# Second products' weights in column pieces, pair 13 combined on the chip, rows read back in pair 14, second norm around two rows

## The chip, the cores and the metric

The kernel runs on one core of one Trainium2 chip. The metric is the device time of one execution in microseconds (us). The kernel before took 1079.23, 1079.86 and 1081.11 us in three runs, median 1079.86 us. The engines are TensorE (PE, its weight loads PEld), VectorE (DVE), ScalarE (ACT), GpSimd (POOL) and SyncE (SP), which here only issues DMAs.

## The reference, cut to what matters

One encoder layer over 512 tokens of 1024 columns in float32: three token mixers, a projection, a first LayerNorm, a mixture of 32 experts, a second LayerNorm. The change lies in the experts and the second norm:

```python
lg = (xt @ wg) + bg; gsel = argmax(lg); p_top = softmax(lg)[gsel]     # one of 4 groups
top_l, top_i = top_k(le_of_that_group, 2)                             # two of its 8 experts
wts = softmax(top_l) * p_top
hdn = silu(xb @ w1[e]) * (xb @ w3[e]); yb = hdn @ w2[e]               # 1024 -> 512 -> 1024
y[token] += yb * wts                                                  # two experts a token
x = LN(alpha * x + y) * ln2_g + ln2_b
```

Each expert has w1 and w3 (1024x512) and w2 (512x1024), 2 MB each. All 32 experts are loaded: 96 blocks, 201 MB.

## The kernel before, in words

Experts go in 16 pairs. A pair's 2x64 token slots stand side by side on TensorE's columns, `q` being the expert of the pair. The blocks come in the order of `seq`: w1 of pair p, w2 of pair p-1, w3 of pair p; at the end w1 and w3 of pair 15, then w2 of 14, then w2 of 15. SP issues their DMAs in that order into a ring of seven slots, each block into the slot that the block seven before it leaves (`load_expert`, L1026; `loads`, L1020). The last eight blocks are loaded in pieces (L1055 to L1060): halves, and four column pieces of w2 of pair 15. In DRAM a w2 block is one row of 4 x 1024 numbers a partition, so a piece of 256 columns is four runs of 1 KB, a piece of 512 columns four runs of 2 KB.

For each pair `pr` (loop L1530) the code emits: `first_product` with w1 (`gate`; between its matmuls 3 and 4 of eight the four transposes of the pair before, `second_product`, L1328), `product` of the pair before with its w2 in two halves of 512 columns (L1413), `put_rows` (POOL scatters that pair's rows to `yd` in DRAM, L1405), `first_product` with w3 (`up`), `gated` (ACT L1321, DVE L1322). Every second pair gathers the next four experts' tokens (`onehots`, `gather`). `XG`, `xnh`, `xnl` are the tokens' rows and their gathered form; `yacc` is the sum for each token.

Pairs 0 to 13 go through `yd`. After pair 14's `gated` stand `overflow()` (a branch over all engines at L1343, not taken here, for experts with more than 64 tokens) and `collect()`: POOL reads `yd` back in eight DMAs of 512 KB (L1279) into the place of `xnh` and `xnl`, and DVE adds each, weighted, to `yacc` (L1282). Pairs 14 and 15 don't go through DRAM: `back` turns the weighted one-hot matrix `Pw` (PE L1314, DVE L1316, L1317), `product` evacuates as a high and a low part (ACT L1422, DVE L1423), and `combine` multiplies them by the one-hots into token order (L1434), which DVE adds to `yacc` (L1438, or L1443 with a sum for the norm). Pair 14's second half is combined within the same accumulation as pair 15's pieces 2 and 3.

The second norm: ACT squares each piece of each token tile t (L1449; the very last tile on DVE, L1446, L1447), `second_scale` makes mean and 1/sd (L1472 to L1475), and `second_norm` scales (ACT L1484), multiplies by the gain `g2` (DVE L1485), adds the offset `b2` (L1487: half of them on POOL, half on DVE) and sends the half row out (SP L1488). `second_rows` (L1457) spreads gain and offset over 128 partitions with 16 fp32 products of 128 columns on PE before pair 15's `up`.

A scheduler of the framework sets each engine's order: by the place in the code, but an instruction that its own timing says could run in a gap is drawn ahead. Each engine then runs its list in order.

Of the kernel before, what the change touches and what calls it, by code (L numbers as in the profile page):

```python
# [72 lines left out]
def _host(inp):  # L73
# [83 lines left out]
def body(tc, T):  # L157
# [847 lines left out]

    def block(i):

        if i == 7:
            return lambda n: lambda c, cs=slice(None): quarter(i, c)[:, cs]
        if i == 8:  # L1010
            return lambda n: lambda c, *cs: quarter(i, c // 2)[:, c % 2 * 512:c % 2 * 512 + 512]
        return lambda n: lambda c, cs=slice(None): reg(slot(i), n, 4096 // n)[:, c, cs]
# [13 lines left out]
    def load_expert(i=None):  # L1026
        if i is None:
            i = nl_[0]
            nl_[0] += 1
        if i < len(seq):  # L1030
            o = slot(i)
            if i == 6:
                pass
            elif i in (7, 8):

                if i == 8:
                    for p in range(4):
                        for k in (7, 8):
                            sp.dma_start(quarter(k, p), T[seq[k][0]][seq[k][1]][:, 1024 * p:1024 * p + 1024])
            elif 9 <= i <= 20:  # L1040

                lone = i in (9, 14)
                old = i - 7 - (i < 14)
                wide = 1024 if seq[old][0] == "moe_w2" else 4096
                if lone or i % 2 == (i < 14):
                    m = wide // (4 if i < 12 else 2)
                    for o in range(0, wide, m):
                        for k in (i,) if lone else (i - 1, i):
                            view = lambda v: v.rearrange("p (f n) -> p f n", n=wide)[:, :, o:o + m]
                            sp.dma_start(view(reg(slot(k), 4096)), view(T[seq[k][0]][seq[k][1]]))  # L1050
            elif i < len(seq) - 8:
                return sp.dma_start(reg(o, 4096), T[seq[i][0]][seq[i][1]])
            elif i % 2:

                n = 1024 if seq[i][0] == "moe_w2" else 4096  # L1055
                for cs in PIECES if i == len(seq) - 1 else [slice(0, n // 2), slice(n // 2, n)]:
                    for k in (i - 1, i):
                        sp.dma_start(reg(slot(k), 4096 // n, n)[..., cs] if n < 4096 else reg(slot(k), n)[:, cs],
                                     T[seq[k][0]][seq[k][1]].rearrange("p (f n) -> p f n", n=n)[..., cs]
                                     if n < 4096 else T[seq[k][0]][seq[k][1]][:, cs])  # L1060
# [235 lines left out]
    def first_product(pr, w, between=None):  # L1296

        so = 128 * (pr % 2)
        ph = pt("as", 2)
        for c in range(8):  # L1300
            if c == 4 and between:
                between()
            for q in range(2):
                pe.matmul(ph[64 * q:64 * q + 64], XG[:, c, so + 64 * q:so + 64 * q + 64], w[q](8)(c),  # L1304
                          start=(c == 0), stop=(c == 7), tile_position=(0, 64 * q))
        return ph
# [24 lines left out]
    def overflow():  # L1331
# [6 lines left out]
        wv = reg(slot(place[14, "moe_w3", 1]), 4096)  # L1338
# [4 lines left out]
        with tc.If(nv > 0), tc.For_i(0, nv, 1):  # L1343
# [34 lines left out]
            w2 = wv.rearrange("p (f n) -> p f n", f=4)  # L1378
            for hf in range(2):
                cs = slice(hf * 512, hf * 512 + 512)  # L1380
                py = pt("pj", 3)[:64]
                for f in range(4):
                    pe.matmul(py, ht[:, f], w2[:, f, cs], start=(f == 0), stop=(f == 3))
# [11 lines left out]
    n2 = [reg(slot(place[15, "moe_w1", 1]) + 1024 * i, 1024) for i in range(2)]  # L1395
    g2, b2 = n2
# [11 lines left out]
    def product(pr, cs, w, PT_=None, ws=None):  # L1408

        py = pt("pj", 3)[:, :cs.stop - cs.start]  # L1410
        for f in range(4):
            for q in range(2):
                pe.matmul(py[64 * q:64 * q + 64], hT[pr % 2][:, f, 64 * q:64 * q + 64], w[q](4)(f, cs),  # L1413
                          start=(f == 0), stop=(f == 3), tile_position=(0, 64 * q))
        if pr < 14:
            if cs.start:
# [8 lines left out]
    def combine(pr, cs, PT_, ws):  # L1425

        terms = [(PT_, v) for v in (yb14 if pr == 14 else yb)]
        if pr == 15 and cs.start >= 512:
            terms = [(turned_[14][0], v) for v in yb14] + terms
        for t in range(4):  # L1430
            pc = (pt("as", 2), pt("ao", 1), pt("as", 2), pt("g", 2))[t]
            pc = pc[:, :cs.stop - cs.start]
# [6 lines left out]
            else:  # L1439

                k = PIECES.index(cs)
                n = cs.stop - cs.start
                dve.scalar_tensor_tensor(ya, pc, 1.0, ya, op0=OP.mult, op1=OP.add, accum_out=bnp[:, t, k, 1:2])  # L1443
                if k == len(PIECES) - 1 and t == 3:
                    d = sil[1][:, (t % 2) * n:(t % 2) * n + n]
                    dve.tensor_scalar(d, ya, -float(n), bnp[:, t, k, 1:2], op0=OP.mult, op1=OP.add)  # L1446
                    dve.scalar_tensor_tensor(d, d, 1.0, d, op0=OP.mult, op1=OP.mult, accum_out=bnp[:, t, k, 2:3])  # L1447
                else:
                    act.activation(junk[:, :n], ya, AF.Square, scale=-float(n), bias=bnp[:, t, k, 1:2],  # L1449
                                   accum_out=bnp[:, t, k, 2:3])  # L1450
                if k == len(PIECES) - 1:
                    second_scale(t)
        if pr == 15 and k == len(PIECES) - 1:
            for t in range(4):
                second_norm(t)

    def second_rows():  # L1457

        for i in range(4):
# [4 lines left out]
            act.activation(n2[i // 2][:, 512 * (i % 2):512 * (i % 2) + 512], p.rearrange("p a b -> p (a b)"), AF.Copy)  # L1464
# [4 lines left out]

    def second_scale(t):  # L1470
# [4 lines left out]
        dve.scalar_tensor_tensor(sm[:, t, 0:1], mv[:, t, 0:1], -1.0 / n, mv[:, t, 1:2], op0=OP.mult, op1=OP.mult)  # L1475

    def second_norm(t):
        for hf in range(2):
            cs = slice(hf * 512, hf * 512 + 512)
            v = yacc[:, t, cs]  # L1480
            if t == 0 and hf == 0:
                dve.tensor_scalar(v, v, mv[:, t, 1:2], sm[:, t, 0:1], op0=OP.mult, op1=OP.add)  # L1482
            else:
                act.activation(v, v, AF.Identity, scale=mv[:, t, 1:2], bias=sm[:, t, 0:1])  # L1484
# [45 lines left out]
    for pr in range(16):  # L1530
# [9 lines left out]
        after = second_rows() if pr == 15 else None  # L1540
        with tc.issue_after(after.ins) if after else nullcontext():
            up = first_product(pr, w[2:4])
        gated(sil[pr % 2], gate, up)
        if pr >= 14:
            turned_[pr] = back(pr)
        if pr == 14:
            overflow()
            collect()
        loads(pr, "moe_w3")
        if pr % 2 and pr < 15:  # L1550
            for t in range(4):
                onehots(pr // 2 + 1, t)
                if pr == 13:
                    weighted(7, t)
# [3 lines left out]
        if pr == 0:  # L1558
            overflow_places()
    evacuated = turned_slots(15)()  # L1560
# [3 lines left out]
    product(14, halves[0], blocks(14)[4:], *turned_[14])  # L1564
    combine(14, halves[0], *turned_[14])
    product(14, halves[1], blocks(14)[4:], *turned_[14])
    for i in range(len(PIECES) + 1):
        if i < len(PIECES):
            product(15, PIECES[i], blocks(15)[4:], *turned_[15])
        if i:  # L1570
            combine(15, PIECES[i - 1], *turned_[15])
    ctx.close()
# [16 lines left out]
```

## Time and profile before

| | us |
|---|---|
| three runs, lowest / median / highest | 1079.23 / 1079.86 / 1081.11 |
| the profiled execution | 1079.46 |
| its span | 1077.5 |
| PE / DVE / ACT / POOL busy | 994.0 / 442.5 / 315.7 / 198.6 |

The profiled execution's time is 1.96 us above its span, and 0.40 us under the median. Times in rows are microseconds from the start of the span. "Busy" of PE counts overlapping matmuls once; the distance of two starts is the better measure of its pace. A row of DMA queues tells packets, MB and the share of 16 DMA engines' time that the packets took. `q1` is SP's queue (weights), `q0` POOL's (rows of `yd`).

### The profile page before, as it was taken

Reading aid. Unit: us, or ns where it says so; the run is one execution under the profiler, and the core shown is the slowest. Engines: PE = TensorE matmul, PEld = TensorE weight load, DVE = VectorE, ACT = ScalarE, POOL = GpSimd, SP = SyncE. Lnnn points to the kernel's source line nnn. Section 1 sums busy time; section 2 is a strip of 40 time slices with the busy share of each in tenths; the row PEclk is TensorE's granted clock in tenths of the full one; section 3 lists DMA queues with packets and bytes.
Section 4 is the critical chain, followed back from the end, with each engine's and each line's share of the span. In section 5 each row is a group of like instructions: output and inputs, shape, how many; then the busy total and the mean of one; then the engine's idle time right before and its main releaser. Section 6 shows DMA issues by size and latency. Waiting matters only on the chain. (4 is left out here: it accounts for less than half of the span.)

```text
span 1077.5 us, 13175 instructions
## 1 busy us (share of the span) xinstructions
PE 994.0 (92%) x5118; PEld 646.1 (60%) x5118; DVE 442.5 (41%) x950; ACT 315.7 (29%) x655; POOL 198.6 (18%) x184
## 2 busy tenths in 40 slices
PE   7989996999999999999998999899989898989973
PEld 5778775977677788888775344434443443334432
DVE  5767893256763533334484221222020210201157
ACT  6873231255653332244133010101010100101115
POOL 1531651222232100233042400000000000000102
PEclk9999998999999999999998999999999999999987
DMA  9422213311114223435465999999999999999982
GB/s 340 165 91 69 84 74 83 113 56 44 59 40 155 81 78 117 196 118 206 175 234 212 382 396 422 428 405 418 429 428 429 428 427 427 428 427 425 404 309 78
DMA packets 52048, 266.04 MB, mean 247 GB/s; under 512 B 15228, under 2 KB 19964, under 8 KB 34832
## 3 DMA queue, kind: packets, MB, share of 16 engines
q1 hardware_dynamic: 47696, 254.67, 59.9%
q0 software_dynamic: 3424, 8.02, 1.9%
q10 hardware_dynamic: 864, 2.49, 0.7%
q8 instruction: 41, 0.67, 0.2%
q14 instruction: 23, 0.19, 0.0%
HBM read 254.13 MB, written 14.61 MB: 249 GB/s over the span
## 5 line engine op out<-in xcount | busy, mean ns | idle before, releaser
L1304 PE MATMUL as<-m,m 128*64 128x512 f32 x1024 | 245.8, 608 | 12.9 <-DMA m<-moe_w 12.9
L1304 PEld LDWEIGHTS as<-m,m 128*64 128x64 f32 x1024 | 77.1, 140 | 154.8 <-issue 133.1
L373 PE MATMUL pj<-m_4096r,m_2048r 128*128 128x512 f32 x400 | 158.2, 396 | 4.4 <-POOL m_2048r L268 2.4
L371 PE MATMUL pj<-m_4096r,m_1024r 128*128 128x512 f32 x400 | 161.0, 402 | 0.0
L372 PE MATMUL pj<-m_4096r,m_1024r 128*128 128x512 f32 x400 | 157.3, 393 | 0.0
L1413 PE MATMUL pj<-m,m 128*64 128x512 f32 (+1 forms) x544 | 128.6, 581 | 5.3 <-DMA m<-moe_w 5.3
L268 DVE TENSOR_TENSOR m_2048r<-m,m_1024r 128x1024 fp32r<-128x1024 f32 x67 | 76.4, 1140 | 98.6 <-ACT m_1024r L267 98.4
L267 ACT ACTIVATE m_1024r<-m 128x512 fp32r<-128x512 f32 (+1 forms) x74 | 68.3, 923 | 138.1 <-PE pj L372 119.8
L1413 PEld LDWEIGHTS pj<-m,m 128*64 128x64 f32 x544 | 45.6, 140 | 79.4 <-issue 67.6
L373 PEld LDWEIGHTS pj<-m_4096r,m_2048r 128*128 128x128 f32 x400 | 75.6, 189 | 21.5 <-POOL m_2048r L268 3.3
L371 PEld LDWEIGHTS pj<-m_4096r,m_1024r 128*128 128x128 f32 x400 | 75.7, 189 | 19.6 <-issue 4.3
L1417 DVE COPY m<-pj 128x512 f32<-128x512 f32 x14 | 9.7, 692 | 186.8 <-PE pj L1413 153.6
L372 PEld LDWEIGHTS pj<-m_4096r,m_1024r 128*128 128x128 f32 x400 | 75.7, 189 | 14.4 <-issue 0.2
L1405 POOL DMA_INDIRECT yd<-m,m x14 | 13.5, 966 | 370.9 <-DVE m L1417 304.2
L1190 PE MATMUL g<-m_1024r,m_4096r 128*128 128x256 f32 x232 | 58.6, 293 | 0.0
L1191 PE MATMUL g<-m_1024r 128*128 128x256 f32 x232 | 56.9, 284 | 0.0
L754 POOL TENSOR_SCALAR m<-m,m 128x128 f32<-128x128 f32 (+3 forms) x32 | 35.8, 1127 | 91.6 <-DVE m L753 85.7
L1290 ACT ACTIVATE m<-g,m 128x256 f32<-128x256 f32 x29 | 16.4, 564 | 121.1 <-PE g L1191 73.5
L1322 DVE TENSOR_TENSOR m<-m,as 128x512 f32<-128x512 f32 x16 | 11.0, 687 | 99.0 <-PE as L1304 99.0
L1190 PEld LDWEIGHTS g<-m_1024r,m_4096r 128*128 128x128 f32 x232 | 44.3, 191 | 6.7 <-issue 6.5
L1329 ACT ACTIVATE m<-g 128x512 f32<-128x512 f32 x16 | 9.6, 597 | 126.4 <-PE g L1328 126.4
L1191 PEld LDWEIGHTS g<-m_1024r 128*128 128x128 f32 x232 | 44.5, 192 | 0.0
(372 smaller groups left out, 1501.3 us busy)
## 6 DMA issues: line engine op xcount, KB each, us to landing
m<-moe_w SPq DMA_DIRECT2D x73, 2048.0 KB, 22.0
m<-wm SPq DMA_DIRECT2D x33, 1024.0 KB, 4.8
m<-moe_w SPq DMA_DIRECT2D x30, 1024.0 KB, 13.7
m<-moe_w SPq DMA_DIRECT2D x32, 512.0 KB, 7.7
yd<-m SPq DMA_DIRECT2D x4, 1024.0 KB, 8.2
m<-wo SPq DMA_DIRECT2D x2, 2048.0 KB, 10.3
m<-yd POOLq DMA_DIRECT2D x8, 512.0 KB, 12.5
m<-xT SPq DMA_DIRECT2D x8, 256.0 KB, 5.5
```

What stands on the lines that cost most here:

```text
L267: act.activation(r32(hi), src, AF.Copy)
L268: lo_engine[0].tensor_tensor(r32(lo), src, hi, op=OP.subtract)
L371: pe.matmul(out, r32(wh(c)), r32(mh(c)), start=(c == 0), stop=False)
L372: pe.matmul(out, r32(wh(c)), r32(ml(c)), start=False, stop=False)
L373: pe.matmul(out, r32(wl(c)), r32(mh(c)), start=False, stop=(c == n - 1))
L754: pool.tensor_scalar(s_[:, :n], s_[:, :n], st[:, 1:2], None, op0=OP.mult)
L1190: pe.matmul(o, r32(xnh[:, t, c * 128:c * 128 + 128]), r32(Pm[:, t]), start=(t == 0), stop=False)
L1191: pe.matmul(o, r32(xnl[t][:, c * 128:c * 128 + 128]), r32(Pm[:, t]), start=False, stop=(t == 3))
L1290: act.activation(XG[:, c], o, AF.Identity, scale=ln1g[:, c:c + 1], bias=ln1b[:, c:c + 1])
L1304: pe.matmul(ph[64 * q:64 * q + 64], XG[:, c, so + 64 * q:so + 64 * q + 64], w[q](8)(c), start=(c == 0), stop=(c == 7), tile_position=(0, 6 ...
L1405: pool.indirect_dma_start(out=yd, out_offset=bass.IndirectOffsetOnAxis(ap=tabs.bitcast(I32)[:, pr, 0:1], axis=0), in_=ybf[pr % 2], in_offs ...
L1413: pe.matmul(py[64 * q:64 * q + 64], hT[pr % 2][:, f, 64 * q:64 * q + 64], w[q](4)(f, cs), start=(f == 0), stop=(f == 3), tile_position=(0, ...
```

## The change

w2 stands in DRAM as four pieces of 256 columns, each one contiguous run of 4 KB a partition; every load of a part of a block is now contiguous. Pair 0's second product runs in four pieces. Pair 13 no longer goes through `yd`: it is turned (`back(13)`) and combined on the chip, in pair 14's place of the loop, with two halves of eight matmuls and eight DVE adds. `overflow` moves from pair 14 to pair 12. `collect` is cut in two: the reads are issued at the end of pair 13 (behind its `gather`), the additions stand at the end of pair 14. A DMA of 8 KB brings gain and offset as two rows (`gb2`). `second_rows` spreads the gain alone; `back(15)` goes ahead of `up`. At the end pair 14's product runs in four pieces, and each half of pair 14 is combined by itself.

In the second norm the gain is multiplied into `yacc` piece by piece before the scale is known (`gained`), and the scale -mean/sd and a row of ones are turned on PE, and multiplied by the two rows: `offset - mean/sd * gain` comes from PE in PSUM, and one DVE instruction finishes a half row. ACT squares all 16 pieces; the last four squares, the scales and the norms are emitted in turn.

```diff
-        a["moe_w2"][0].reshape(32, 4, 128, 1024).transpose(0, 2, 1, 3).reshape(32, 128, 4096))
+        a["moe_w2"][0].reshape(32, 4, 128, 4, 256).transpose(0, 2, 3, 1, 4).reshape(32, 128, 4096))
+    d["ln2gb"] = np.ascontiguousarray(np.concatenate([a["ln2_g"], a["ln2_b"]], axis=0))
...
-                n = 1024 if seq[i][0] == "moe_w2" else 4096
-                for cs in PIECES if i == len(seq) - 1 else [slice(0, n // 2), slice(n // 2, n)]:
+                n = 1024 if i > len(seq) - 5 else 2048
+                for o in range(0, 4096, n):
                     for k in (i - 1, i):
...
+                        sp.dma_start(reg(slot(k), 4096)[:, o:o + n], T[seq[k][0]][seq[k][1]][:, o:o + n])
...
         for t in range(4):
             for j in range(2):
                 pool.dma_start(rows[j][t], yd[512 * j + 128 * t:512 * j + 128 * t + 128])
+        yield
...
-        if pr == 15 and cs.start >= 512:
-            terms = [(turned_[14][0], v) for v in yb14] + terms
...
+    def gained(k, ts=range(4)):
+        for t in ts:
+            ya = yacc[:, t, PIECES[k]]
+            dve.tensor_tensor(ya, ya, g2[:, PIECES[k]], op=OP.mult)
...
     def second_scale(t):
...
+        yield
         dve.reciprocal(mv[:, t, 1:2], mv[:, t, 1:2])
+        dve.scalar_tensor_tensor(ms[:, t, 0:1], mv[:, t, 0:1], -1.0 / n, mv[:, t, 1:2], op0=OP.mult, op1=OP.mult)
+        p = pt("g", 2)[0:2, 0:128]
+        pe.transpose(p, ms[:, t], ident)
+        act.activation(rows2[:, t], p, AF.Copy)
+        yield
     def second_norm(t):
         for hf in range(2):
             cs = slice(hf * 512, hf * 512 + 512)
+            p = pt("pj", 3)
+            pe.matmul(p, rows2[:, t], gb2[:, cs], start=True, stop=True)
             v = yacc[:, t, cs]
-            dve.tensor_tensor(v, v, g2[:, cs], op=OP.mult)
-            e = pool if hf == 0 else dve
-            e.tensor_tensor(v, v, b2[:, cs], op=OP.add)
+            dve.scalar_tensor_tensor(v, v, mv[:, t, 1:2], p, op0=OP.mult, op1=OP.add)
             sp.dma_start(ov[:, t, cs], v)
...
         if 0 < pr < 15:
-            for cs in halves:
-                product(pr - 1, cs, blocks(pr - 1)[4:])
-            put_rows(pr - 1)
+            for cs in PIECES if pr == 1 else halves:
+                product(pr - 1, cs, blocks(pr - 1)[4:], *turned_.get(pr - 1, ()))
             loads(pr - 1, "moe_w2")
+            if pr < 14:
+                put_rows(pr - 1)
+            else:
+                for cs in halves:
+                    combine(pr - 1, cs, *turned_[pr - 1])
+        if pr == 15:
+            second_rows()
+            turned_[pr] = back(pr)
...
-        if pr == 14:
+        if pr == 12:
             overflow()
-            collect()
...
+        if pr == 13:
+            rows_ = collect()
+            next(rows_)
+            pool.dma_start(gb2, T["ln2gb"])
+        if pr == 14:
+            drain(rows_)
+    last = [lambda cs=cs: product(14, cs, blocks(14)[4:], *turned_[14]) for cs in PIECES]
+    last[0]()
     evacuated = turned_slots(15)()
...
+    last[1]()
+    last[2]()
     combine(14, halves[0], *turned_[14])
+    last[3]()
     for i in range(len(PIECES) + 1):
         if i < len(PIECES):
             product(15, PIECES[i], blocks(15)[4:], *turned_[15])
+        if i == 0:
+            combine(14, halves[1], *turned_[14])
+        else:
             combine(15, PIECES[i - 1], *turned_[15])
+            if 1 < i < len(PIECES):
+                gained(i - 2)
...
+    for t in range(4):
+        next(scales[t])
+        if t < 2:
+            gained(2, (t + 2,))
+        gained(3, (t,))
+        next(scales[t])
+        if t:
+            second_norm(t - 1)
+    second_norm(3)
```

## Rows read from the trace of the kernel before

**Rows 1.** Windows: us, busy and count of each engine, granted clock, DMA share, GB/s.
```profile
900.00:950.00 50.00, 44.96 (x232) 20.56 (x231) 9.15 (x20) 4.73 (x9) 1.92 (x2) 1.00 1.01 427
...
1027.50:1033.10 5.60, 0.00 (x0) 0.00 (x0) 4.07 (x5) 0.00 (x0) 0.00 (x0) 0.77 1.03 396
1034.20:1049.20 15.00, 14.22 (x71) 6.60 (x70) 7.09 (x11) 3.93 (x6) 0.00 (x0) 0.90 0.84 274
1048.00:1050.00 2.00, 2.00 (x16) 1.36 (x12) 0.69 (x2) 0.63 (x2) 0.00 (x0) 1.00 0.03 12
1049.20:1059.40 10.20, 10.20 (x81) 8.05 (x80) 6.89 (x33) 8.39 (x28) 0.00 (x0) 1.00 0.00 0
1059.40:1074.00 14.60, 0.00 (x0) 0.00 (x0) 14.12 (x30) 7.44 (x17) 6.59 (x4) 0.68 0.29 108
1074.00:1077.50 3.50, 0.00 (x0) 0.00 (x0) 0.00 (x0) 0.00 (x0) 0.00 (x0) 0.50 0.41 152
```

**Rows 2.** Timeline of PE, pairs 14 and 15: start, us, what, count, idle before.
```profile
989.66 0.66 PE L1314 MATMUL g<-m,m 128*128 128x128 f32 x4
...
1013.03 0.74 PE L1328 MATMUL g<-m,m 128*128 128x128 f32 x4 [1.97 <-PEq L1343]
...
1015.27 1.81 PE L1463 MATMUL g<-m 128*128 128x128 f32 x8
1016.91 1.06 PE L1463 MATMUL pj<-m 128*128 128x128 f32 x8
...
1018.79 7.09 PE L1304 MATMUL as<-m,m 128*64 128x512 f32 x32
...
1033.19 1.09 PE L1328 MATMUL g<-m,m 128*128 128x128 f32 x4 [5.72 <-DVE m L1322]
1034.20 5.17 PE L1413 MATMUL pj<-m,m 128*64 128x512 f32 x16
1040.15 0.50 PE L1434 MATMUL as<-m_1024r,m_512r 128*128 128x512 f32 x1 [0.78 <-ACT m_1024r L1422]
...
1041.89 0.40 PE L1434 MATMUL g<-m_1024r,m_512r 128*128 128x512 f32 x1
...
1050.39 1.95 PE L1413 MATMUL pj<-m,m 128*64 128x256 f32 x16
...
1058.76 0.64 PE L1434 MATMUL g<-m_1024r,m_512r 128*128 128x256 f32 x4
```

**Rows 3.** Timeline of POOL and DVE around the rows read back from `yd`.
```profile
1013.41 4.40 POOL L1279 DMA_DIRECT2D m<-yd  x8 [13.64 <-PEq L1343]
1021.04 1.28 DVE L1282 SCALAR_TENSOR_TENSOR m<-m,m,m 128x1024 f32<-128x1024 f32 x1 [16.05 <-DMA m<-yd]
...
1032.36 0.68 DVE L1322 TENSOR_TENSOR m<-m,as 128x512 f32<-128x512 f32 x1
```

**Rows 4.** DMA queues in 960 to 980 and in 985 to 1005.
```profile
q1 hardware_dynamic: 576, 8.41, 98.6%
...
q0 software_dynamic: 85, 0.20, 2.5%
```

**Rows 5.** DMA queues in 1020 to 1030, then in 1036 to 1048.
```profile
q0 software_dynamic: 727, 2.65, 67.4%
q1 hardware_dynamic: 690, 1.38, 36.3%
...
q1 hardware_dynamic: 3472, 3.47, 88.2%
```

**Rows 6.** Timeline of DVE and ACT in the last stage.
```profile
1042.24 0.68 DVE L1438 TENSOR_TENSOR m<-m,ao 128x512 f32<-128x512 f32 x1
...
1050.54 0.41 DVE L1443 SCALAR_TENSOR_TENSOR m<-ao,m 128x256 f32<-128x256 f32 x1
...
1052.44 0.51 ACT L1449 ACTIVATE m<-m,m 128x256 f32<-128x256 f32 x1
...
1068.76 4.01 DVE L1485 TENSOR_TENSOR m<-m,m 128x512 f32<-128x512 f32 x3
```

More of the change, by code (lines that the diff above doesn't have):

```diff
@@ L1004, in quarter, with w2_columns @@
         return reg(RING[2] + 1024 * k if i == 7 else woh[1][k], 1024)
+    def w2_columns(v, f, cs):
+        k0, k1 = cs.start // 256, cs.stop // 256
+        return v[:, k0, f] if k1 == k0 + 1 else v[:, k0:k1, f]
     def block(i):
-        if i == 7:
-            return lambda n: lambda c, cs=slice(None): quarter(i, c)[:, cs]
+        if seq[i][0] == "moe_w2":
+            if i == 7:
+                return lambda f, cs: shaped(quarter(i, cs.start // 256), 4, 256)[:, f]
+            return lambda f, cs: w2_columns(reg(slot(i), 4, 4, 256), f, cs)
         if i == 8:
-            return lambda n: lambda c, *cs: quarter(i, c // 2)[:, c % 2 * 512:c % 2 * 512 + 512]
-        return lambda n: lambda c, cs=slice(None): reg(slot(i), n, 4096 // n)[:, c, cs]
+            return lambda c: quarter(i, c // 2)[:, c % 2 * 512:c % 2 * 512 + 512]
+        return lambda c: reg(slot(i), 8, 512)[:, c]
     def blocks(pr):
@@ L1042, in load_expert @@
                 lone = i in (9, 14)
-                old = i - 7 - (i < 14)
-                wide = 1024 if seq[old][0] == "moe_w2" else 4096
                 if lone or i % 2 == (i < 14):
-                    m = wide // (4 if i < 12 else 2)
-                    for o in range(0, wide, m):
+                    m = 4096 // (4 if i < 12 else 2)
+                    for o in range(0, 4096, m):
                         for k in (i,) if lone else (i - 1, i):
-                            view = lambda v: v.rearrange("p (f n) -> p f n", n=wide)[:, :, o:o + m]
-                            sp.dma_start(view(reg(slot(k), 4096)), view(T[seq[k][0]][seq[k][1]]))
+                            sp.dma_start(reg(slot(k), 4096)[:, o:o + m], T[seq[k][0]][seq[k][1]][:, o:o + m])
             elif i < len(seq) - 8:
@@ L1382, in overflow @@
                 for f in range(4):
-                    pe.matmul(py, ht[:, f], w2[:, f, cs], start=(f == 0), stop=(f == 3))
+                    pe.matmul(py, ht[:, f], w2_columns(w2, f, cs), start=(f == 0), stop=(f == 3))
                 act.activation(r32(yb[0][:64, cs]), py, AF.Copy, scale=ws)
@@ L1393, in overflow @@
             dve.tensor_scalar(cnt[:, 1:2], cnt[:, 1:2], 64.0, None, op0=OP.add)
-    n2 = [reg(slot(place[15, "moe_w1", 1]) + 1024 * i, 1024) for i in range(2)]
-    g2, b2 = n2
+    g2 = reg(slot(place[15, "moe_w1", 1]), 1024)
+    gb2 = reg(MSB, 1024)[0:2]
     ov = T["out"].rearrange("(t p) d -> p t d", p=128)
@@ L1412, in product @@
             for q in range(2):
-                pe.matmul(py[64 * q:64 * q + 64], hT[pr % 2][:, f, 64 * q:64 * q + 64], w[q](4)(f, cs),
+                pe.matmul(py[64 * q:64 * q + 64], hT[pr % 2][:, f, 64 * q:64 * q + 64], w[q](f, cs),
                           start=(f == 0), stop=(f == 3), tile_position=(0, 64 * q))
-        if pr < 14:
-            if cs.start:
+        if pr < 13:
+            if cs.start % 512 or cs.start and cs.stop - cs.start == 512:
                 dve.tensor_copy(ybf[pr % 2][:, cs], py)
@@ L1427, in combine @@
         terms = [(PT_, v) for v in (yb14 if pr == 14 else yb)]
-        if pr == 15 and cs.start >= 512:
-            terms = [(turned_[14][0], v) for v in yb14] + terms
+        n = cs.stop - cs.start
         for t in range(4):
-            pc = (pt("as", 2), pt("ao", 1), pt("as", 2), pt("g", 2))[t]
-            pc = pc[:, :cs.stop - cs.start]
+            pc = pt(*((("pj", 3), ("ao", 1), ("pj", 3), ("g", 2)) if pr == 13 else
+                      (("as", 2), ("ao", 1), ("as", 2), ("g", 2)))[t])[:, :n]
             for i, (m, v) in enumerate(terms):
@@ L1439, in combine @@
             else:
-                k = PIECES.index(cs)
-                n = cs.stop - cs.start
+                k = cs.start // n
                 dve.scalar_tensor_tensor(ya, pc, 1.0, ya, op0=OP.mult, op1=OP.add, accum_out=bnp[:, t, k, 1:2])
[L1444 to L1455, printed above, removed]
+                act.activation(junk[:, :n], ya, AF.Square, scale=-float(n), bias=bnp[:, t, k, 1:2],
+                               accum_out=bnp[:, t, k, 2:3])
+    def gained(k, ts=range(4)):
+        for t in ts:
+            ya = yacc[:, t, PIECES[k]]
+            dve.tensor_tensor(ya, ya, g2[:, PIECES[k]], op=OP.mult)
     def second_rows():
-        for i in range(4):
+        for i in range(2):
             p = pt("g", 2, 4, 128) if i % 2 else pt("pj", 3, 4, 128)
@@ L1468, in body @@
     junk = sil[0]
+    ms = small(4, 2)
+    rows2 = reg(slot(place[15, "moe_w1", 1]) + 1024, 4, 128)[0:2]
     def second_scale(t):
@@ L1535, in body @@
         if 0 < pr < 15:
-            for cs in halves:
-                product(pr - 1, cs, blocks(pr - 1)[4:])
-            put_rows(pr - 1)
+            for cs in PIECES if pr == 1 else halves:
+                product(pr - 1, cs, blocks(pr - 1)[4:], *turned_.get(pr - 1, ()))
             loads(pr - 1, "moe_w2")
-        after = second_rows() if pr == 15 else None
-        with tc.issue_after(after.ins) if after else nullcontext():
-            up = first_product(pr, w[2:4])
+            if pr < 14:
[6 more added lines that the diff above has]
+            turned_[pr] = back(pr)
+        up = first_product(pr, w[2:4])
         gated(sil[pr % 2], gate, up)
-        if pr >= 14:
+        if pr in (13, 14):
             turned_[pr] = back(pr)
-        if pr == 14:
+        if pr == 12:
             overflow()
-            collect()
         loads(pr, "moe_w3")
@@ L1552, in body @@
                 onehots(pr // 2 + 1, t)
-                if pr == 13:
-                    weighted(7, t)
+                if pr > 10:
+                    weighted(pr // 2 + 1, t)
             gather()
@@ L1563, in body @@
     dve.memset(bnp[:, :, :, 0:1], float(PIECES[0].stop))
-    product(14, halves[0], blocks(14)[4:], *turned_[14])
+    dve.memset(ms[:, :, 1:2], 1.0)
+    last[1]()
+    last[2]()
     combine(14, halves[0], *turned_[14])
-    product(14, halves[1], blocks(14)[4:], *turned_[14])
+    last[3]()
     for i in range(len(PIECES) + 1):
@@ L1569, in body @@
             product(15, PIECES[i], blocks(15)[4:], *turned_[15])
-        if i:
+        if i == 0:
+            combine(14, halves[1], *turned_[14])
+        else:
             combine(15, PIECES[i - 1], *turned_[15])
+            if 1 < i < len(PIECES):
+                gained(i - 2)
+    scales = [second_scale(t) for t in range(4)]
+    gained(2, (0, 1))
+    for t in range(4):
[7 more added lines that the diff above has]
+    second_norm(3)
     ctx.close()
```

16 lines of the change are left out of this document (4 added, 12 removed).

## The prediction

> **What bounds the kernel now.** I read the windows first, by stage, then PE's timeline at the end, then the DMA queues. In the expert stage the weights bound: from 900 to 950 the 16 DMA engines are full (share 1.01, 427 GB/s) while PE is busy for 44.96 of 50 us [rows 1]. So work added to PE, DVE, ACT or POOL before the last pairs is free up to about 5 us in 50, and so is the branch's stop of PE (1.97 us). The DMA bytes are not free anywhere.
>
> At the end the bound changes three times [rows 1]. From 1027.5 to 1033.1 PE does nothing and the DMA engines are full. From 1034.2 PE is the bound: 14.22 of 15.0 us, then 10.20 of 10.20, while the DMA share falls to 0.84 and 0. From PE's last product (1059.4, its last row in [rows 2]) to 1074.0 DVE is busy for 14.12 of 14.60, and 3.5 us follow for the last row's way out. The chain of waits shows only this last part. So three things count: when PE can start the last products (call it S, 1034.20 in [rows 2]), how long it needs from S to its end E (25.2 us to 1059.40), and what follows E (18.1 us). These give the span of 1077.5; the profiled execution took 1.96 us more, and it lies 0.40 us under the median.
>
> **Step 1, the stream and S.** PE's 5.72 us are a wait for `gated(15)` [rows 2], which stood on DVE behind six additions of rows from `yd`: the first waited for 16.05 us, and L1322 ran at 1032.36 though `up` had ended at 1025.9 [rows 2, 3]. The reads had been issued at 1013.41, behind the branch [rows 3]. In the new order they go out near 981, behind pair 13's gather, so this wait goes, and with it the branch's 1.97 us and half of `second_rows`. What is late next is the weights themselves: the 4.19 MB of reads pass ahead of w3 of pair 15 instead of behind it.
>
> When do the weights end? Their last data moved at 1048 (from there the DMA share is 0.03 [rows 1]). Packets of 16 KB move at 8.41 MB / (0.986 x 20 us) = 426 GB/s [rows 4], of 4 KB at 2.65 / 6.74 = 393, of 2 KB at 1.38 / 3.63 = 380, of 1 KB at 3.47 / 10.6 = 328 [rows 5]. Pair 15's w2 (4.19 MB) goes from 1 KB to 4 KB packets: 12.8 to 10.7 us, -2.1. Pair 14's, from 2 KB to 4 KB: -0.4. Pair 13's scatter is no more: -0.5 (2.5% of 20 us [rows 4]). Up to three early blocks get larger packets: at most 6.3 MB x (1/380 - 1/426) = -1.8 us, nothing if slots were late there; I take -0.5. The data then end at 1044.5. Behind w3 of pair 15 lie 8.39 MB at 393 GB/s, 21.3 us, so its data end at 1023.2; with 1 us until this is known and half of `up` (7.09 us [rows 2]) behind it, S is 1027.8 at best. PE waits for weights in this stretch. After the idle stretch at 1027.5 its granted clock was 0.77 over that window, so part of it at the lower level of 1.2 GHz, where four fp32 products of 128 columns take 1.64 us (1015.27 to the next group's start at 1016.91) instead of 0.89 (1.06 less the same overlap of 0.17) [rows 2]. One such stretch in `gate` or `up` costs about 2 us. I take S = 1030, bounds 1027.8 and 1033.
>
> Hidden in this stage: pair 13's two halves of combining (2 x 2.1 us of PE, and eight adds of 0.6 on DVE [rows 2, 6]), its turn (0.66), the extra one-hots, pair 0's quarter pieces (4 x 1.9 instead of about 7.1, +0.5), the branch at pair 12. The cover is the 5 us in 50 and the longer DMA time of pairs 14 and 15. SP passes the branch with four or five blocks of 2 MB still in flight (4.9 us each at 427), so the stream should not run dry there; a dry stream would cost its whole idle time, 0 to 5 us, and I take 0.
>
> **Step 2, S to E.** Eight pieces at 1.9 (1.95 with the last one's end) are 15.2; pair 14's halves 2 x 2.14 (eight products from 1040.15 to 1042.29) 4.3; pair 15's four combinings of half the columns 4 x 1.07, 4.3; the turn 0.7; the last evacuation's wait, mostly covered by the piece before, 0.2 (0.78 uncovered) [rows 2]. Sum 24.7, 0.5 less than before. DVE and ACT keep up, just: a piece of pair 15 costs DVE some 3.0 us with the gain (four adds with sum at 0.34 apart, four products as long, an evacuation), PE 2.95, ACT 3.05. E = 1054.7.
>
> **Step 3, E to the end.** POOL leaves. In [rows 6] three products by the gain take 4.01 us on DVE beside POOL, against 0.60 a piece when DVE is alone (four adds of 0.68 start 0.60 apart). From E on DVE's own sum is now 1.4 (four sums) + 2.6 (eight gains of 256 columns) + 1.8 (small ones) + 8 x 0.62 = 10.8 us. But two other chains are longer. ACT squares all 16 pieces at some 0.65 (0.51 and a read of the sum, [rows 6]) and starts when the first sums of pair 15 exist, 7.4 us before E; with two evacuations that is 11.3 us, so its last square ends at E + 3.9. Root, reciprocal, product, transposition and copy, each a hop of 0.2 to 0.4, follow; I take 1.7. At E + 5.6 PE begins eight fp32 products of 512 columns. Their moving operand has two rows, but 512 columns are four times 128: 0.89 each at 2.4 GHz and 1.64 at 1.2 [rows 2]. PE has stood still for 5 us by then, as before 1033. I take two at the lower level, two half and half, four at the upper: 3.3 + 2.5 + 3.6 = 9.4; transpositions between them 0.5; the last DVE instruction 0.7; the way out 3.5. The sum is E + 19.7. Bounds: all at the upper level E + 17.4, all at the lower E + 23.4, and DVE alone, if PE kept ahead, E + 14.3.
>
> The rule of the Trainium skill that speaks against this step is in "TensorE: Matmul & The Clock Gate", section "Why this matters for your kernels": idle gaps between bursts of matmuls bring the clock back to its lower level. The trace agrees (granted 0.68 over 1059.4 to 1074.0, 0.50 after [rows 1]). It changes the mix of the eight products, no bound.
>
> **Sum.** 1054.7 + 19.7 = 1074.4, against 1077.5: S -4.2, S to E -0.5, behind E +1.6. With 1.96 the profiled execution would take 1076.4; on the scale of the median 0.4 more: 1076.8.
>
> **Rivals.**
>
> *The reads hold `gated(14)` (slower).* DVE's additions stand in the code behind `gated(14)`, but they need only pair 13's combining, some 7 us earlier, so the scheduler may draw them ahead; it did so with pair 14's turn, which runs at 989.66 inside pair 13's product [rows 2]. On the chip the reads are slow there: when both queues had work they moved one packet for one (727 and 690 [rows 5]). 1024 packets of 4 KB are 64 for each DMA engine; beside 16 KB packets one takes 0.62 + 0.17 us, beside 8 KB ones 0.31 + 0.17. From 981, 22 pass with w3 of pair 14 until 998, the other 42 with the halves of w1 and w3 of pair 15 until about 1018. If six additions stand ahead, as they did before L1322, the sixth ends near 1012 and w1's second half comes no earlier than that: nothing lost. If all eight do, `gated(14)` ends at 1020.5, then come the turn, half of `gate` (3.5), `second_rows` and `back` (3.4), `up` (7.1) and one stretch at the lower level: S = 1037, E = 1061.7, and with the same tail and the same 2.4 a time of 1083.8. It decides from the point at which L1322 of pair 14 starts later than 1014. For it: the same instructions stopped DVE before. Against: it takes the last two of eight. Chance 0.2.
>
> The skill's "DMA: Bandwidth & Descriptors", section "Queues, rings and completion order", has it that an engine alternates between queues packet by packet; the trace's 727 to 690 agrees. With a share by bytes the reads would be done near 1001, and this rival would be gone.
>
> *The tail is DVE's.* The matmuls stay ahead because the clock holds, or ACT is not behind. Then E + 16: 1070.7, time 1073.1. For it: DVE is the engine that is busy there now (14.12 of 14.60 [rows 1]). Against: 0.50 granted after such a pause. Chance 0.2.
>
> *Nothing comes of it.* The stream's gain is eaten by PE at the lower level through both `gate` and `up`: S = 1033, E = 1057.7, time 1079.8. That includes that larger packets don't do what they say, for then S is 2 us later and no more. Chance 0.13.
>
> **How the numbers follow.** Forecast 0.47, with 1073.5 to 1079 as its own range. Less than 0.2% (2.2 us) can't be told from no change here: within 1077.7 to 1082.0. Faster: 0.41 of the forecast, 0.20 of the DVE tail, 0.02 of the others: 0.63. Same: 0.06, 0.02 and 0.12: 0.20. Slower: most of the first rival and a little else: 0.17. The range goes from 1071 (the DVE tail with S near its best) to 1084.
>
> **What would show it.** Right: no PE wait of 5 us for L1322; the DMA share at zero from about 1045; PE's last product of pair 15 near 1054.7; the first product with two rows 5 to 6 us behind it, the first two 1.6 us long, the later 0.9; POOL idle at the end. Wrong: L1322 of pair 14 or 15 behind a read; a PE gap in `gate(15)` over 5 us that no weight explains; a tail from E under 17 us, which would say that ACT or PE is not its bound; a DMA share under 0.95 between 700 and 1030.

## The result and the profile after

The changed kernel is slower: 1087.51 us median (1085.49 to 1088.80, 4 runs) against 1080.36 of the kernel before on the same chip (1079.23 to 1081.11, 4 runs), ratio 1.0065, 95% interval 1.0046 to 1.0084. Forecast were 1076.8 and a range of 1071 to 1084.

The profiled run of the changed kernel took 1088.80 us, its span 1087.0. Single profiles differ by some 2 to 3 us before the experts begin, so positions of two runs are compared from the first expert product of each (the common scale). These are the groups of that line in the first microseconds of the experts, before and after (durations min/median/max in ns, first and last start):

```profile
L1304 PE MATMUL as<-m,m x16: 592/593/1115, 581.8 to 585.6; 128*64 128x512 f32 x16
```

```profile
L1309 PE MATMUL as<-m,m x16: 592/592/1117, 584.2 to 587.9; 128*64 128x512 f32 x16
```

On that scale, with S the start of pair 14's second products (one product that was drawn ahead isn't counted where PE waits behind it) and E the end of PE's last combine:

| | before | after | difference | forecast |
|---|---|---|---|---|
| S (1034.20 less 581.8; 1032.85 less 584.2) | 452.4 | 448.65 | -3.75 | -4.2 |
| S to E | 25.2 | 29.7 | +4.5 | -0.5 |
| E to the end | 18.1 | 24.5 | +6.4 | +1.6 |
| sum | 495.7 | 502.85 | +7.15 | -3.1 |

The sum happens to equal the difference of the medians (7.15); the profiled run of the changed kernel was the slowest of its four. S came nearly as forecast, and both stretches behind it were lost. One profile places S to some 2 us only: in the four runs below whose edits, but for clearing memory, lie behind S (clock held up, one pass, written order, 128 rows) it is 448.0, 448.0, 449.0 and 451.0. The windows of the changed kernel that answer to [rows 1] (us, busy time and count by engine, granted clock, DMA share, GB/s):

```profile
900.00:950.00 50.00, 42.51 (x206) 18.16 (x205) 5.25 (x11) 4.65 (x8) 1.93 (x2) 0.97 1.01 427
...
1020.00:1032.85 12.85, 12.85 (x65) 5.21 (x66) 4.96 (x5) 2.17 (x4) 0.00 (x0) 1.00 1.01 405
1032.85:1047.90 15.05, 14.58 (x96) 8.64 (x94) 6.34 (x12) 3.87 (x7) 0.00 (x0) 1.00 0.80 320
1047.90:1062.50 14.60, 14.47 (x90) 8.75 (x86) 9.42 (x38) 8.52 (x27) 0.00 (x0) 1.00 0.01 3
1062.50:1067.00 4.50, 0.18 (x2) 0.08 (x1) 4.50 (x23) 3.14 (x12) 0.00 (x0) 0.97 0.01 2
1067.00:1083.50 16.50, 15.73 (x20) 5.05 (x19) 6.92 (x16) 1.56 (x6) 0.00 (x0) 0.50 0.27 102
1083.50:1087.00 3.50, 0.00 (x0) 0.00 (x0) 0.19 (x1) 0.00 (x0) 0.00 (x0) 0.50 0.32 120
```

PE's stop before the last products is gone (12.85 of 12.85 where [rows 1] had 0.00 of 5.60). Behind S the stream still has 0.80 x 15.05 = 12.0 us of full work, so it ends near 1044.9; before, 0.84 x 15.0 put it at 1046.8. On the common scale that is 4.3 us earlier; forecast were 3.5. The last window but one is the surprise: PE, not DVE, is busy nearly throughout, at a granted clock of 0.50 (1.2 GHz). PE's timeline answers to [rows 2] (start, us, what, count, idle before):

```profile
963.90 1.11 PE L1309 MATMUL as<-m,m 128*64 128x512 f32 x1 [6.42 <-DMA m<-moe_w]
...
1032.85 0.59 PE L1418 MATMUL pj<-m,m 128*64 128x256 f32 x2
...
1049.55 0.65 PE L1418 MATMUL pj<-m,m 128*64 128x256 f32 x2
1050.13 0.39 PE L1438 MATMUL as<-m_1024r,m_512r 128*128 128x256 f32 x1
...
1050.59 0.28 PE L1438 MATMUL g<-m_1024r,m_512r 128*128 128x256 f32 x1
1050.80 1.94 PE L1418 MATMUL pj<-m,m 128*64 128x256 f32 x14
1052.67 0.39 PE L1438 MATMUL as<-m_1024r,m_512r 128*128 128x256 f32 x1
...
1062.25 0.28 PE L1438 MATMUL g<-m_1024r,m_512r 128*128 128x256 f32 x1
1066.85 0.37 PE L1480 MATMUL g<-m,m 128*2 128x128 f32 x1 [4.32 <-DVE m L1478]
...
1067.69 3.78 PE L1489 MATMUL pj<-m,m 2*128 2x512 f32 x4
...
1075.71 7.19 PE L1489 MATMUL pj<-m,m 2*128 2x512 f32 x8
```

Two things are to be seen. A piece of 256 columns no longer runs as x16 in 1.95 us [rows 2] but torn, x2 and, behind four products of a combining, x14. And the norm's products (two instructions each) take 1.7 to 1.9 us for 512 columns, from the first to the last. POOL and DVE, for [rows 3]:

```profile
988.74 0.61 POOL L1283 DMA_DIRECT2D m<-yd  x1 [12.47 <-PE g L1195]
```

```profile
1010.83 4.86 DVE L1287 SCALAR_TENSOR_TENSOR m<-m,m,m 128x1024 f32<-128x1024 f32 x4
1016.91 0.69 DVE L1327 TENSOR_TENSOR m<-m,as 128x512 f32<-128x512 f32 x1 [1.21 <-PE as L1309]
```

The reads go out 24.7 us earlier than before (1013.41 in [rows 3]; 27.1 on the common scale), and pair 14's gating waits for PE, not for a read.

### The profile page after: what moved, and what is told of

Same layout as the page of the kernel before. It is cut to its first block, busy times and chain, and to the rows that moved or that the text cites. A ratio compares the mean times of both kernels' runs of the same rounds, so it can differ in the third digit from the quotient of the medians.

```text
span 1087.0 us, 13368 instructions
## 1 busy us (share of the span) xinstructions
PE 1014.2 (93%) x5198; PEld 655.0 (60%) x5198; DVE 453.1 (42%) x985; ACT 312.6 (29%) x656; POOL 192.3 (18%) x180
## 4 chain that ended last, share of the span: by engine, by line
PE 71%; DMA 12%; DVE 10%; ACT 3%; issue 2%; POOL 1%; SPq 0%; POOLq 0%; DVEq 0%; ACTq 0%
PE as L1309 17%; DMA m<-moe_w 11%; PE pj L1418 8%; PE pj L373 8%; PE pj L375 8%; PE pj L374 7%; DVE m L604 3%; PE g L1194 2%; PE g L1195 2%; PE pj L1489 1%; PE as L747 1%; DVE m L606 1%; PE ao L778 1%; PE pj L1203 1%; PE as L766 1%
## 5 line engine op out<-in xcount | busy, mean ns | idle before, releaser
L1418 PE MATMUL pj<-m,m 128*64 128x512 f32 (+1 forms) x608 | 131.1, 544 | 3.7 <-DMA m<-moe_w 3.7
L1418 PEld LDWEIGHTS pj<-m,m 128*64 128x64 f32 x608 | 51.0, 140 | 75.4 <-issue 61.8
L1422 DVE COPY m<-pj 128x512 f32<-128x512 f32 (+1 forms) x14 | 9.1, 653 | 178.3 <-PE pj L1418 145.1
L1327 DVE TENSOR_TENSOR m<-m,as 128x512 f32<-128x512 f32 x16 | 11.0, 688 | 99.0 <-PE as L1309 99.0
```

## The experiments

Each ran beside the kernel before on the same chip. The sets of runs differ, so two runs are compared by their ratios to before (changed kernel 1.0065), where 0.001 is 1.1 us. In the code, `lastp` and `lastc` hold the last matmul emitted so far by a product or a combining.

### The tail

**Old norm.** `second_rows`, `second_scale`, `second_norm` and the squares as before the change, the rest as changed.

> The changed kernel with the second norm of the kernel before (four broadcast rows, ACT, DVE and POOL at the end, no two-row products). Theory A, that the two-row products at the lower clock make the tail: from PE's last combine to the end about 18 us as before, against 24.5 in the changed kernel; two more rows to broadcast cost PE 1 to 2 us before the last products; the time falls from 1087.5 to 1082 to 1084. Rival B, that the tail is long for a reason that lies before PE's last combine (late sums, DVE behind): the tail stays at 22 us or more and the time within 1086 to 1089.

1085.53 us, ratio 1.0035 (1.0020 to 1.0051): about 3 us less than the changed kernel. E to the end took 19.2 us against 24.5. So the tail is at fault, and not for anything that lies before E (theory A). It is less gain than the tail alone would give, and less than expected, since S came 3.3 us later, counted from the gate of pair 14; two more rows are spread there, and whether they cost all of it stays open.

**Clock held up.**

```diff
+    with tc.issue_after(lastc[0].ins):
+        for _ in range(28):
+            warm[0] = pe.matmul(o, r32(turned_[15][0][:, 0:128]), r32(yb[0][:, 0:512]), start=True, stop=True)
```

> The changed kernel, and 28 full-row one-pass products of 512 columns (their result is not read) put on PE between its last combine and the first transposition of the norm, some 6 us at the upper level. Theory A1, that the pause of 4.3 us alone sets the clock down: it stays at 1.00 through the eight two-row products, each 512 columns takes 0.9 us instead of 1.7, the norm's products start at most 1.5 us later, and the tail is 18 to 19.5 us instead of 24.5: time 1082 to 1084. Rival A2, that products with two rows do not hold the upper level: the clock is 1.00 up to the first of them, falls to 0.50 while they run, and the tail is 22 to 24.5: time 1085 to 1088.

1085.22 us, ratio 1.0046 (1.0028 to 1.0064). Windows from the added products on:

```profile
1059.80:1066.30 6.50, 6.46 (x28) 5.26 (x29) 4.71 (x26) 3.37 (x12) 0.00 (x0) 1.00 0.00 1
1066.30:1070.90 4.60, 4.35 (x12) 1.49 (x10) 2.17 (x3) 0.69 (x3) 0.00 (x0) 1.00 0.21 78
1070.90:1078.60 7.70, 7.60 (x10) 2.58 (x9) 3.11 (x6) 0.27 (x1) 0.00 (x0) 0.50 0.42 157
```

The clock stays at 1.00 over the pause, and the first four products have it: they take 0.86 us each, the last four, at 0.50, 1.70. It falls to 0.50 while PE goes on (7.60 of 7.70 us busy). The tail is 23.7 us. A1, the pause alone, falls: products of two rows did not hold the upper level.

**128 rows.** Both operands of the same products filled up with 126 rows of zeros (`gb2` as shown, `rows2` in the same way).

```diff
-    gb2 = reg(MSB, 1024)[0:2]
+    gb2 = reg(MSB, 1024)
```

> The changed kernel with the two rows of the norm's products filled up with zero rows to 128 rows on both operands; the pause before them stays. Same columns, so the same 0.9 and 1.7 us for 512 columns at the two levels. A1 (only the pause counts): no change, clock 0.50 to the end or, as with two rows, not back up; tail 24.5, time 1086 to 1089. A2 (the rows count): the clock comes back while the products run, as it did in the kernel before between 1030.5 and 1037.3, some 7 us after the pause; the last four products take about 0.9, the tail is 20.5 to 22.5: time 1083 to 1086.

1081.57 us, ratio 0.9996 (0.9981 to 1.0010), no slower than before. Windows from E on:

```profile
1064.70:1069.00 4.30, 0.01 (x1) 0.00 (x0) 4.30 (x22) 3.13 (x12) 0.00 (x0) 0.70 0.01 2
1069.00:1073.20 4.20, 4.00 (x6) 1.46 (x7) 2.08 (x11) 1.02 (x4) 0.00 (x0) 0.50 0.00 0
1073.20:1078.90 5.70, 5.65 (x15) 2.21 (x13) 4.49 (x7) 0.53 (x2) 0.00 (x0) 1.00 0.62 233
```

The pause is the same 4.3 us, the products have as many columns, and the clock is back at 1.00 while they run. The tail is 18.9 us, shorter than expected, since six products and not four ran at the upper level. The rows made the difference (A2), zeros among them.

One could still suspect the moment at which the clock falls in the pause: with 128 rows it fell early (0.70 over the pause), in the changed kernel only at its end (0.97). The run with the written order, further down, has two rows and an early fall. Its windows, the pause and then the products:

```profile
1056.44:1061.00 4.56, 0.09 (x1) 0.08 (x1) 4.36 (x23) 3.80 (x14) 0.00 (x0) 0.75 0.01 2
1061.00:1077.40 16.40, 15.79 (x20) 5.05 (x19) 6.83 (x17) 1.57 (x6) 0.00 (x0) 0.50 0.26 99
```

The clock stayed at 0.50 to the end. So it did in the two further runs with the two exact rows (pair 13's `up`, branch at pair 10).

**One pass.** The same products of two rows with both operands rounded to the short format.

```diff
-            pe.matmul(p, rows2[:, t], gb2[:, cs], start=True, stop=True)
+            pe.matmul(p, r32(rows2[:, t]), r32(gb2r[:, cs]), start=True, stop=True)
```

> The changed kernel with the norm's eight products in one pass: both operands of two rows rounded to the short format, otherwise the same. Theory A (PE's eight products are the bound of the tail): a product of 512 columns takes 0.43 us at the lower level instead of 1.7, DVE's eight instructions of 0.6 follow one another without waits, the tail is 15 to 16.5 us instead of 24.5: time 1078 to 1080. Rival B (ACT's squares or DVE make the tail): less than 2 us gained, time above 1085.

1077.43 us, ratio 0.9971 (0.9956 to 0.9987), tail 15.8. DVE's timeline, the norm's eight instructions (L1491, there L1492):

```profile
1065.00 5.62 DVE L1492 SCALAR_TENSOR_TENSOR m<-m,m,pj 128x512 f32<-128x512 f32 x8 [0.35 <-PE pj L1490]
```

They follow one another without a wait; in the changed kernel each waited 0.96 to 1.63 us for PE. PE was the bound (A). Its eight products now lie within 5.3 us, transpositions included, where they took 15.2, and DVE is the bound although the clock is still 0.50.

### From S to E

**Written order.** Each `product` and `combine` from pair 14 on stands inside an order edge behind the one before.

```diff
+    def then(f, *a):
+        with tc.issue_after(lastp[0].ins):
+            f(*a)
...
-    last[1]()
+    then(last[1])
```

> The changed kernel with the products and combinings of the last two pairs held on PE in the order in which the code writes them, so that no piece has one of its 256-column products drawn ahead of the combining before it. Theory C (the torn pieces and groups): an intact piece takes 1.88 us against 2.45 torn, some five of them 2.7 us, and the groups of combining some 1.5 us less: from the first product of pair 14 to PE's last combine 25 to 26 us instead of 29.7, time 1083 to 1084.5 against 1087.5. Rival D (the drawn products fill a wait for the evacuation, which the fixed order lays bare, 0.5 us or more a piece): 28.5 us or more, time within 1086 to 1089.

1082.59 us, ratio 1.0014 (0.9999 to 1.0029). S to E is 25.1 us (1031.31 to 1056.44). PE's timeline:

```profile
1045.85 1.95 PE L1418 MATMUL pj<-m,m 128*64 128x256 f32 x16
1047.72 0.50 PE L1438 MATMUL as<-m_1024r,m_512r 128*128 128x256 f32 x2
```

Theory C holds, D falls: no wait for an evacuation came to light, and the 4.6 us are back. A torn piece costs 0.57 us because its two column halves run side by side only while both have work. In the intact piece the instructions of the halves start in pairs, within 0.01 us; in the x14 six pairs do, and the last two instructions run alone, 0.22 us apart. So the x14 takes 1.94, as long as x16, since one half still has all its products to do, and the x2 ahead comes on top (1049.55 to 1050.13 is 0.58, 1050.80 to 1052.67 is 1.87, against 1.88 intact). Five of them are 2.8. Of the other 1.7, 0.6 are waits of PE that the written order doesn't have (0.60 us without a product from S to E, now 0.02); the 1.1 that remain are put down to the combinings, torn in their turn.

### Up to S

**Pair 13's `up` behind pair 12's second products.**

```diff
-        up = first_product(pr, w[2:4])
+        with tc.issue_after(lastp[0].ins) if pr == 13 else nullcontext():
+            up = first_product(pr, w[2:4])
```

> The changed kernel with the up products of pair 13 held behind the second products of pair 12 on PE; in the changed kernel one of them stood ahead and PE waited 6.4 us for its weights while those of the second products had been there 4.9 us earlier. Theory E2: that wait falls to about 1.5 us, the gate of pair 14 starts 4 to 5 us earlier, the last products 2.5 to 4: time 1083.5 to 1085. Rival F (the weights of pair 15 decide): less than 1 us, above 1086. Rival G: the wait comes back as long in front of the up products: no change.

1084.73 us, ratio 1.0026 (1.0014 to 1.0038); on the common scale S and the end come 2.8 us earlier. PE's timeline:

```profile
954.54 7.09 PE L1418 MATMUL pj<-m,m 128*64 128x512 f32 x32 [0.25 <-ACT m L1334]
...
964.10 2.37 PE L1309 MATMUL as<-m,m 128*64 128x512 f32 x10 [1.62 <-DMA m<-moe_w]
...
1019.45 8.27 PE L1309 MATMUL as<-m,m 128*64 128x512 f32 x29 [2.21 <-DMA m<-moe_w]
```

The wait of 6.42 us is 1.62, and the gate of pair 14 starts 6.9 us earlier on the common scale. But 1.5 us of this and of the 2.8 lie ahead of the gate of pair 13, which the edit doesn't touch. Counted from that gate, pair 14's gate comes 5.4 us earlier and S only 1.3: a new wait of 2.21 us for the weights of pair 15 stands in `up`, with a lower clock behind it (0.86 over 1020 to 1030). E2 and F each hold in part: the drawn product cost PE its lead, and the stream takes over as soon as PE has it again.

**Branch at pair 10**, behind `own_rows`.

> The changed kernel with the branch for the overfull experts at pair 10 instead of pair 12. Theory E (PE's stops around the branch, 3.3 and 6.4 us with the clock at the lower level behind each, are never won back, since PE is without a wait from there on): three pairs under the weights' bound win them back, the gate of pair 14 starts 4 to 6 us earlier and the last products 2.5 to 4, time 1083.5 to 1085. Rival F (the weights of pair 15 set the start of the last products anyway): gate earlier, last products less than 1 us earlier, time above 1086.

1089.55 us, ratio 1.0064 (1.0040 to 1.0089): no gain, though the gate of pair 14 starts 4.7 us earlier. Windows:

```profile
910.00:920.00 10.00, 9.69 (x48) 3.33 (x46) 5.96 (x21) 1.79 (x3) 0.00 (x0) 1.00 0.85 360
920.00:940.00 20.00, 20.00 (x122) 11.69 (x118) 6.19 (x14) 3.45 (x6) 0.96 (x1) 1.00 0.90 362
```

The stream lost 0.15 x 10 + 0.10 x 20 = 3.5 us there, and the last weights end some 4 us later on the common scale. E falls, F holds by a way that it had not named.

**The branch at pair 10 again**, on the kernel of three edits (next section), with pair 11's `up` held behind pair 10's second products too.

> The kernel of the three edits with the branch at pair 10, and pair 11's up held behind pair 10's second products as pair 13's is behind pair 12's. Theory L (the branch at pair 10 gained nothing because products drawn ahead of it made PE late to release slots, and the stream ran dry for 3.5 us): the stream keeps a share of 1.00 from 900 to 940, the last products start as in the three edits, set by the weights of pair 15: time 1071 to 1073. Rival M (SP's stop at the branch itself makes the stream run dry there): share 0.85 to 0.95 in some 20 us, 1073.5 to 1076.

1072.75 us, ratio 0.9909 (0.9889 to 0.9928), as with the branch at pair 12 (0.9910). Windows:

```profile
900.00:920.00 20.00, 18.89 (x112) 11.02 (x110) 4.51 (x11) 2.25 (x5) 0.96 (x1) 1.00 1.01 429
920.00:940.00 20.00, 19.86 (x92) 6.55 (x90) 2.79 (x7) 2.23 (x4) 0.96 (x1) 1.00 1.00 428
```

The share stays full. So it was the drawn products (L): PE waited for their weights ahead of the branch, second products came late, and SP had no slot to load into. A stop of SP at the branch is not to be seen in the stream.

### The three edits together, and the change undone in them

**Three edits**: written order, pair 13's `up`, one pass.

> Three edits together on the changed kernel: the last products in the written order, pair 13's up behind pair 12's second products, the norm's products in one pass. If A, C and E2 are right and their gains add: 1087.5 less 10, 3.5 and 3 is 1071 (1069.5 to 1073); if the weights set the start of the last products (F): 1073 to 1075; if only the norm counts: 1077.

1071.87 us, ratio 0.9910 (0.9886 to 0.9933): faster than both kernels, and as expected from the sum. By the ratios the gains are 10.2, 5.5 and 4.2 us singly and 16.8 together, so they nearly add.

**Exact norm in it**, 128 rows in place of one pass.

> The last products in the written order and pair 13's up behind pair 12's second products, with the norm's products exact as in the changed kernel but with 128 rows (zeros) instead of two. If the rows set the clock, as it looked in the run with 128 rows alone: the tail is 18.5 to 19.5 us against 24.5 with two rows and 16.1 with one pass, the clock back at 1.00 some 4 us into the products: time 1074 to 1075.5. If that clock had come by chance: 1079 to 1081.

1077.37 us, ratio 0.9947 (0.9928 to 0.9966), later than expected by some 2 us in its median; S to E is 25.1, the tail 19.1, as expected. The difference lies ahead of the edit: in its profile the gate of pair 13 starts 2.9 us later on the common scale than in the three edits, and from there to S both take 87.8. PE's timeline, the norm:

```profile
1062.50 3.73 PE L1489 MATMUL pj<-m,m 128*128 128x512 f32 x4
...
1066.18 1.88 PE L1489 MATMUL pj<-m,m 128*128 128x512 f32 x4
...
1068.01 3.60 PE L1489 MATMUL pj<-m,m 128*128 128x512 f32 x8
```

The first two products take 1.8 to 1.9 each, the other six 0.9. So the clock that came back in the run with 128 rows alone had not come by chance.

**Old layout of w2 in it.**

```diff
-        a["moe_w2"][0].reshape(32, 4, 128, 4, 256).transpose(0, 2, 3, 1, 4).reshape(32, 128, 4096))
+        a["moe_w2"][0].reshape(32, 4, 128, 1024).transpose(0, 2, 1, 3).reshape(32, 128, 4096))
```

> The kernel of the three edits (1071.9) with the second products' weights in DRAM in whole rows as before the change, so 1 and 2 KB packets for the last pairs instead of 4 KB. Theory H (the packets are worth what the forecast said, and the stream sets the start of the last products): data of the last weights end 2.5 to 3 us later; the last products of pair 15 wait for them, or their start comes up to 0.5 us later since w3 of pair 15 stands ahead of most of it: time 1072.5 to 1075. Rival I (larger packets don't matter): within 1071 to 1072.5.

1077.14 us, ratio 0.9947 (0.9928 to 0.9966): by the ratios 4.0 us more than the three edits (5.3 in the medians), later than either theory had it. Windows of the old layout, then of the three edits alone:

```profile
1040.00:1046.00 6.00, 5.55 (x38) 3.60 (x40) 3.36 (x6) 0.62 (x2) 0.00 (x0) 1.00 1.00 331
1046.00:1050.00 4.00, 4.00 (x28) 2.50 (x24) 1.74 (x4) 0.95 (x2) 0.00 (x0) 1.00 0.73 248
```

```profile
1040.00:1046.00 6.00, 6.00 (x43) 3.80 (x40) 3.36 (x6) 1.28 (x3) 0.00 (x0) 1.00 0.58 234
1046.00:1050.00 4.00, 4.00 (x35) 2.84 (x35) 3.84 (x17) 3.21 (x11) 0.00 (x0) 1.00 0.00 0
```

With the DMA engines full (share 1.00) the old layout moves 331 GB/s; the changed kernel moved 401 at that share from 1035 to 1040. PE's timeline with the old layout:

```profile
1032.38 0.65 PE L1423 MATMUL pj<-m,m 128*64 128x256 f32 x2
...
1035.06 1.94 PE L1423 MATMUL pj<-m,m 128*64 128x256 f32 x14 [1.69 <-DMA m<-moe_w]
...
1040.45 1.94 PE L1423 MATMUL pj<-m,m 128*64 128x256 f32 x14 [0.57 <-DMA m<-moe_w]
```

Counted from the gate of pair 13 in each run (944.6 and 941.3), the data end at 104.3 and 102.2. One product of pair 14 starts as early as in the three edits, at 87.8, but then PE waits for pair 14's weights, so that S lies at 90.5 against 87.8, E 3.0 us and the end 2.0 us later. Theory H holds with 2 to 3 us. The other 2.9 us lie before that gate, and the run with the exact norm, which has the new layout, is later there by as much; what of them is the layout stays open.

**Branch and reads back at pair 14 in it.**

> The kernel of the three edits with the branch and the reads of the stored rows back at pair 14, behind the gate and up products. Theory J (the early reads are what the start of the last products gained): the reads are issued some 25 us later, the additions of rows stand in front of the gated product of pair 15 and between the evacuations of pair 14, PE waits 4 us or more for them, time 1076 to 1081. Rival K (the weights set the start anyway, and the additions fit between): time below 1074.

1079.00 us, ratio 0.9973 (0.9955 to 0.9991): by the ratios 6.8 us more than the three edits (7.1 in the medians). PE's waits behind the reads:

```profile
1029.35 0.63 PE L1333 MATMUL g<-m,m 128*128 128x128 f32 x4 [3.66 <-DVE m L1327]
1036.74 0.50 PE L1438 MATMUL as<-m_1024r,m_512r 128*128 128x512 f32 x1 [2.72 <-DVE m_1024r L1428]
...
1046.96 0.49 PE L1438 MATMUL ao<-m_1024r,m_512r 128*128 128x512 f32 x1 [1.85 <-DVE m L1442]
```

DVE, for the first of them:

```profile
1027.33 1.28 DVE L1287 SCALAR_TENSOR_TENSOR m<-m,m,m 128x1024 f32<-128x1024 f32 x1 [5.61 <-DMA m<-yd]
```

This addition stood ahead of L1327, the other seven between the evacuations of pair 14. J holds. Branch and reads went back together, so their shares can't be told apart; the waits shown, 8.2 us, hang on the reads.

## Why the prediction was wrong

**Step 1, the stream and S: right.** S came 3.75 us earlier, against -4.2, the data's end 4.3 against 3.5; the wait for the reads is gone, and undoing a part of the step in the kernel of three edits costs about what it had been given: 2 to 3 us for the packets (given 3.0), some 7 for branch and reads together (given 5.72 and 1.97). With S known to some 2 us from one profile, the closeness of -3.75 to -4.2 is partly luck. Of what was costed at nothing, one item was not: around the branch PE stood for 3.31 and 6.42 us, not 1.97, and from 988.8 to S it was busy without a wait. The cover of 5 us in 50 was gone by then. In S that cost 1.3 us counted from the gate of pair 13, and no more, because the stream is nearly as late.

**Rival one, the reads in front of `gated(14)`: did not happen.** L1327 of pair 14 ran at 1016.91, behind four additions, and waited for PE. That is later than the 1014 that the forecast had named as its sign, without a wait for a read; the sign should have named what L1327 waits for.

**Step 2, S to E: wrong by 5.0 (29.7 us, forecast 24.7).** It failed in taking eight intact pieces at 1.9 and whole groups of combining from [rows 2]. The new order alternates pieces and combinings more often, and at each seam the scheduler may draw a product ahead. The forecast used that habit for the additions in rival one and not for the pieces. Its sum itself was right: 25.1 in the written order, against 24.7. What the torn order cost is 4.6.

**Step 3, E to the end: wrong by 4.8 (24.5 us, forecast 19.7).** The chain up to the first product was sized well (5.2 us, forecast 5.6). The step that failed is the mix of the eight products, "two at the lower level, two half and half, four at the upper", 9.4 us and 0.5 for transpositions: all eight ran at the lower level and took 15.2 with the transpositions between them. The prices of one product were nearly right (0.86 and 1.70 measured with the clock held up, forecast 0.89 and 1.64); the clock was not. That the clock comes back while products run was taken from [rows 2], where the products had 128 rows. With 128 rows it did come back, and the tail was 18.9 and 19.1, against the 19.7 of the forecast. The bound of E + 23.4 had been named, 1.1 too low, and given too little weight. Rival two, the tail by DVE, is what one pass made of it: 15.8, against E + 16.

The rule of the Trainium skill that the forecast weighed, that idle gaps bring the clock down, agrees with the pause. The same page of the Trainium skill, "TensorE: Matmul & The Clock Gate", section "Part 1: The HAM clock gate (the "warmup" mystery)", has the clock follow how busy PE has been recently; by that, products that keep PE busy would have brought it up again. Here PE was busy for 15.73 of 16.50 us at 0.50, and in the run with the clock held up the clock fell to 0.50 out of busy products. The measurements decide: busy time alone, as these profiles count it, does not say it.

With written order, pair 13's `up` held back (which was no part of the forecast) and 128 rows, each stretch comes near its forecast: S -3.3 on the common scale, S to E 25.1, the tail 19.1, and a ratio of 0.9947 (0.9928 to 0.9966) where 1076.8 / 1079.86 = 0.9972 had been forecast.

## What to carry to other kernels

Before pricing a product by another row of the same trace, compare the contraction rows too, not only columns and clock. Where a scheduler may draw instructions ahead, price a new order by its seams, or fix it. A stop of one engine is free only as long as what it holds up releases nothing that the bounding stream needs.

## What was not expected of the hardware

Products of two contraction rows kept PE busy, yet the granted clock stayed at 0.50 for all of their 15.2 us, and fell to 0.50 in the middle of them when it had been held at 1.00; the same products with 126 rows of zeros added brought it back to 1.00, in both runs that had them. Filling up with zeros made the kernel 0.7% faster (ratios 1.0065 and 0.9996).
